# Attention values transposed twice, as fp32 and as fp32r from a DMA's copy, with the scaled difference added

## The chip, the cores and the metric

The kernel runs on one core of one Trainium2 chip, in one launch. The metric is the device time of that core in microseconds (us); lower is better. The core has five engines with queues of their own: PE (TensorE, matmuls; its weight loads are shown apart as PEld), DVE (VectorE), ACT (ScalarE), POOL (GpSimd) and SP (SyncE, which here only issues DMAs). Each engine takes its instructions strictly in the order of its queue and waits on semaphores for the others.

## The reference, cut to what matters

The program is one inference step of a two-layer hybrid encoder: layer 0 is a Mamba-2 mixer with a SwiGLU FFN, layer 1 is banded attention with a SwiGLU FFN. It is computed for 1024 prompt frames and 64 sample frames, which the kernel keeps side by side as 1088 columns. Only the attention of layer 1 matters here:

```python
kp, vp = shared_kv(xp, kv_norm_w, w_kv)          # rmsnorm(x) @ w_kv, split into K and V
qp = (rmsnorm(xp, nw[0]) @ attn_w_q[i]).reshape(bp, -1, ATT_HEADS, ATT_HEAD_DIM)
...
s = jnp.einsum('bqhd,bkhd->bhqk', q, k).astype(jnp.float32) * (ATT_HEAD_DIM ** -0.5) + bias
s = jnp.where(valid, s, -jnp.inf)
p = jax.nn.softmax(s, axis=-1).astype(v.dtype)
return jnp.einsum('bhqk,bkhd->bqhd', p, v)
```

There are 16 heads of 64 features. A query frame sees the frames of its own chunk of 64 and of the 8 chunks before it.

## The kernel before, in words

Everything is kept with features on the 128 partitions and frames along the free dimension. The 1088 columns are cut into three slices (SL) of 384, 384 and 320 columns. The 16 heads are taken as eight pairs j = 0..7; a pair's 128 features fill the partitions. Projections are done with split operands: each fp32 number is a rounded part (fp32r) and a rest, and a unit of projection (`unit`, `passes`, lines 533 to 535) is 8 steps of three matmuls, 24 in all, into one PSUM tile called mm.

For each pair j and slice s there are three units, K, V and Q. The function that empties a unit's PSUM tile is `evk` (line 1910: kf, then its rounded part on ACT and its rest on DVE, lines 1917 and 1918), `evv` (line 1964: vt) or `evq` (line 1936: qf). For V the values have to be turned, since the product of probabilities and values wants frames on the partitions: `v_task` transposes the three 128x128 blocks of vt on PE (line 1953, against the constant ident, into a PSUM tile vtp) and DVE copies the result to Vn (line 1954).

The attention itself goes in blocks of 128 queries, nine for each pair. A block has three steps, each placed by conditions of its own: the scores (lines 2001 and 2002, into PSUM tiles S; DVE adds the bias and finds the minimum at line 2011, ACT takes the exponential at 2016, DVE normalizes at 2017 and 2018), the transposition of the probabilities (line 2032, PSUM tiles ptp, copied out to pT at line 2036 by DVE for one head and ACT for the other), and, once for each slice, `values` (line 2067: po, the product with Vn, for three blocks in a row; ACT empties po at line 2075).

What sets the order. The program is written by a class `Stream` that counts planned time st.t while it writes PE's work: each matmul of a unit adds its planned cost, and side tasks (Python generators) yield a pair (cost, delay): the cost is added to st.t, and the task goes on when st.t has passed by the delay. So PE's queue is written out in full by the program, with attention steps put between the quarters of units. The instructions of the other engines are ordered by a scheduler with priorities: HIP (3000) for the emptying of units (lines 1909, 1935, 1963), ATP (1000) for the softmax steps and the copies to pT, and none for the copy to Vn.

Three resources matter below. The PSUM pool pax has two tiles with the tag ax, which `ax()` hands out in turn: vtp and po are such tiles. The pool nsb has tiles with the tags ssum (3 buffers) and sq (2 buffers), which the norms use before and after the attention. The tag kqv has four buffers, shared by kf, vt and qf. DMAs of the attention stage are all issued from SP's queue.

## Time and profile before

| what | value |
|---|---|
| median of 3 runs (lowest, highest) | 2895.07 us (2892.39, 2895.51) |
| the profiled execution's own time | 2895.43 us |
| its span (first to last instruction) | 2893.7 us |
| mean granted TensorE clock | 0.997 |
| busy PE, DVE, ACT, POOL | 2843.4, 2227.5, 1347.6, 772.8 us |
| attention stage | about 1594 us to 2060 us of the span |

The 1.7 us between the span and the execution's own time lie outside the first and the last instruction. In the rows of a timeline the first column is the start in us from the span's start, the second the duration; matmuls are pipelined, so that the distance from one start to the next, and not the duration, is what one costs. An entry in square brackets is the idle time of the engine before the row and what ended it. L1953 is line 1953 of the kernel.

### The profile page before, as it was taken

Reading aid. Unit: us, or ns where it says so; the run is one execution under the profiler, and the core shown is the slowest. Engines: PE = TensorE matmul, PEld = TensorE weight load, DVE = VectorE, ACT = ScalarE, POOL = GpSimd, SP = SyncE. Lnnn points to the kernel's source line nnn. Section 1 sums busy time; section 2 is a strip of 40 time slices with the busy share of each in tenths; the row PEclk is TensorE's granted clock in tenths of the full one; section 3 lists DMA queues with packets and bytes.
Section 4 is the critical chain, followed back from the end, with each engine's and each line's share of the span. In section 5 each row is a group of like instructions: output and inputs, shape, how many; then the busy total and the mean of one; then the engine's idle time right before and its main releaser. Section 6 shows DMA issues by size and latency. Waiting matters only on the chain. (4 is left out here: it accounts for less than half of the span.)

```text
span 2893.7 us, 57789 instructions
## 1 busy us (share of the span) xinstructions
PE 2843.4 (98%) x22096; PEld 2799.2 (97%) x22096; DVE 2227.5 (77%) x4739; ACT 1347.6 (47%) x2411; POOL 772.8 (27%) x971
## 2 busy tenths in 40 slices
PE   8999999999999999999999999999999999999999
PEld 8999999999999999999998899999999999999998
DVE  7887888886769877787677677777778877787456
ACT  6654646454454222235444555555564322234442
POOL 1343333330123434351024000000032434343012
PEclk9999999999999999999999999999999999999999
DMA  4433333235556555558875422223377454566555
GB/s 135 129 103 99 105 102 106 94 118 159 174 166 175 163 166 170 174 191 273 286 225 177 131 91 76 65 65 90 97 215 215 136 185 147 183 205 203 193 181 160
DMA packets 284791, 443.23 MB, mean 153 GB/s; under 512 B 25697, under 2 KB 231489, under 8 KB 283105
## 3 DMA queue, kind: packets, MB, share of 16 engines
q1 hardware_dynamic: 275232, 423.47, 45.6%
q0 software_dynamic: 3232, 10.56, 2.1%
q10 hardware_dynamic: 6048, 5.51, 0.6%
q8 instruction: 173, 2.83, 0.4%
q14 instruction: 106, 0.86, 0.1%
HBM read 321.34 MB, written 113.63 MB: 150 GB/s over the span
## 5 line engine op out<-in xcount | busy, mean ns | idle before, releaser
L533 PE MATMUL mm<-r,hl 128*128 128x384 f32 (+2 forms) x1672 | 556.2, 333 | 4.1 <-DMA hl<-kscr 2.4
L535 PE MATMUL mm<-r,hl 128*128 128x384 f32 (+2 forms) x1672 | 539.3, 323 | 1.2 <-DVE hl L389 0.7
L534 PE MATMUL mm<-r,hl 128*128 128x384 f32 (+2 forms) x1672 | 539.2, 322 | 0.0
L1428 PE MATMUL px<-r,hl 128*128 128x288 f32 (+1 forms) x1184 | 347.6, 294 | 0.0
L533 PEld LDWEIGHTS mm<-r,hl 128*128 128x128 f32 x1672 | 316.4, 189 | 6.1 <-DMA hl<-kscr 2.6
L535 PEld LDWEIGHTS mm<-r,hl 128*128 128x128 f32 x1672 | 315.3, 189 | 1.9 <-DVE hl L389 1.0
L534 PEld LDWEIGHTS mm<-r,hl 128*128 128x128 f32 x1672 | 316.2, 189 | 0.3
L1427 PE MATMUL px<-r,hl 128*128 128x288 f32 x1056 | 311.1, 295 | 2.8 <-DVE u L1448 1.6
L1429 PE MATMUL px<-r,hl 128*128 128x288 f32 x1056 | 311.4, 295 | 0.0
L389 DVE TENSOR_TENSOR hl<-raw,hl 128x1024 fp32r<-128x1024 f32 (+2 forms) x186 | 209.6, 1128 | 117.1 <-ACT hl L386 116.8
L559 POOL TENSOR_TENSOR ssum<-ssum,sq 128x256 f32<-128x256 f32 (+1 forms) x111 | 125.0, 1127 | 551.3 <-ACT sq L558 536.3
L386 ACT CAST hl<-raw 128x1024 fp32r<-128x1024 f32 (+2 forms) x186 | 177.5, 955 | 116.2 <-PE po L1770 72.3
L1428 PEld LDWEIGHTS px<-r,hl 128*128 128x128 f32 x1184 | 222.5, 188 | 0.0
L1429 PE MATMUL px<-rx,hl 128*128 128x256 f32 x768 | 214.9, 280 | 2.9 <-DVE hl L389 2.9
L1427 PE MATMUL px<-rx,hl 128*128 128x256 f32 x768 | 214.7, 280 | 0.9 <-DVE u L1442 0.9
L1427 PEld LDWEIGHTS px<-r,hl 128*128 128x128 f32 x1056 | 198.8, 188 | 4.6 <-DVE u L1448 2.0
L1429 PEld LDWEIGHTS px<-r,hl 128*128 128x128 f32 x1056 | 198.8, 188 | 0.1
L1768 PE MATMUL po<-r,hl 128*128 128x288 f32 (+1 forms) x682 | 196.7, 288 | 0.0
L1769 PE MATMUL po<-r,hl 128*128 128x288 f32 (+1 forms) x682 | 196.4, 288 | 0.0
L1770 PE MATMUL po<-r,hl 128*128 128x288 f32 (+1 forms) x682 | 196.4, 288 | 0.0
L1428 PE MATMUL px<-rx,hl 128*128 128x256 f32 x640 | 179.0, 280 | 0.0
L2016 ACT ACTIVATE sc<-sc,mx 128x640 f32<-128x640 f32 (+3 forms) x144 | 101.8, 708 | 106.3 <-DVE mx L2011 103.5
(450 smaller groups left out, 8428.9 us busy)
## 6 DMA issues: line engine op xcount, KB each, us to landing
raw<-in_w_f_dram SPq DMA_DIRECT2D x104, 512.0 KB, 4.0
wsum<-in_w_f_dram SPq DMA_DIRECT2D x128, 176.0 KB, 3.7
wscr<-wsum SPq DMA_DIRECT2D x128, 176.0 KB, 3.3
raw<-in_w_in_dram SPq DMA_DIRECT2D x40, 512.0 KB, 3.7
MT<-ascr SPq DMA_DIRECT2D x48, 384.0 KB, 4.3
raw<-in_w_so_dram SPq DMA_DIRECT2D x32, 512.0 KB, 3.8
r<-hscr SPq DMA_DIRECT2D x22, 576.0 KB, 6.0
hl<-kscr SPq DMA_DIRECT2D x11, 1024.0 KB, 6.1
```

Source lines behind the costliest of these rows:

```text
L386: last = self.nc.scalar.copy(h, v)
L389: (eng or self.eng or self.nc.vector).tensor_tensor(lo, v, h, op=ALU.subtract)
L533: PE.matmul(ps[:, :n], h_, xh, start=(first and i == 0), stop=False)
L534: PE.matmul(ps[:, :n], h_, xl, start=False, stop=False)
L535: at_pe[0] = PE.matmul(ps[:, :n], l_, xh, start=False, stop=(last and i == nk - 1))
L559: (eng or G).tensor_tensor(ssum[:, :n], ssum[:, :n], q[:, :n], op=ALU.add)
L1427: PE.matmul(ps, wh, ah[:, k, :], start=(k == 0), stop=False)
L1428: PE.matmul(ps, wh, al[:, k, :], start=False, stop=False)
L1429: at_pe[0] = PE.matmul(ps, wl, ah[:, k, :], start=False, stop=(k == 3))
L1768: PE.matmul(ps[:, :n], wh, xh, start=(k == 0), stop=False)
L1769: PE.matmul(ps[:, :n], wh, xl, start=False, stop=False)
L1770: at_pe[0] = PE.matmul(ps[:, :n], wl, xh, start=False, stop=(k == KH - 1))
```

## The change

Each `v_task` now also copies vt to a second tile vc by a DMA from SBUF to SBUF, waits 4.0 us of planned time, transposes vt as before, transposes vc once more with both operands taken as fp32r (with a copy of the identity matrix in fp32r, made once by ACT) into a second PSUM tile vtr, subtracts Vn from that on DVE, and adds the difference times 1048576 to Vn. The planned cost of a task goes from 0.33 to 0.55. There are 24 such tasks (eight pairs, three slices).

```diff
         def v_task(j, s, vt):
             Vn = kqv[j]["V"][s] = sb2.tile([P, 3, P], F32, tag="Vn", bufs=KBUF, name="Vn")
+            vc = nsb.tile([P, 384], F32, tag="ssum", bufs=3, name="vc")
+            nc.sync.dma_start(vc, vt)
+            if "ident" not in state:
+                state["ident"] = sb2.tile([P, P], F32R, tag="identr", bufs=1, name="identr")
+                A.copy(state["ident"], ident)
+            yield 0, 4.0
             pt = ax("vtp")
             for i in range(3):
                 PE.transpose(pt[:, i * P:(i + 1) * P], vt[:, i * P:(i + 1) * P], ident)
-            V.tensor_copy(Vn, pt[:, :3 * P].rearrange("p (a b) -> p a b", b=P))
-            yield 0.33, 0
+            flat = Vn.rearrange("p a b -> p (a b)")
+            V.tensor_copy(flat, pt[:, :384])
+            pt = ax("vtr")
+            for i in range(3):
+                PE.transpose(rr(pt[:, i * P:(i + 1) * P]), rr(vc[:, i * P:(i + 1) * P]), state["ident"])
+            df = nsb.tile([P, 384], F32, tag="sq", bufs=2, name="df")
+            V.tensor_tensor(df, pt[:, :384], flat, op=ALU.subtract)
+            V.scalar_tensor_tensor(flat, df, 1048576.0, flat, op0=ALU.mult, op1=ALU.add)
+            yield 0.55, 0
             v_done.append((j, s))
```

In the changed kernel the lines after these are 13 higher: 1954 (the copy to Vn) is now 1961, 1953 is 1959, the new transposition is 1964, the subtraction 1966, the scaled addition 1967; 2011 is 2024, 2018 is 2031, 2032 is 2045, 2067 is 2080.

Since the planned delay is longer, the tasks land at other places of PE's queue. PE's queue before, around the product po of a pair's first slice (12 rows of a projection unit stand ahead of the first row; ptp is the transposition of the next block's probabilities):

```order
L535 MATMUL mm<-r,hl 128x384
L2067 MATMUL po<-pT,Vn 64x128 x12
L2032 MATMUL ptp<-ident,sc 128x128 [waits DVE_49]
L2032 MATMUL ptp<-ident,sc 128x128 x3
L2032 MATMUL ptp<-ident,sc 128x128 [waits DVE_49]
L2032 MATMUL ptp<-ident,sc 128x128 x3
```

Here the product itself waits for nothing; the transposition of V for the next pair comes after it, six matmuls further on. PE's queue now, from that transposition on (vtp and vtr are the two transpositions, S the scores of the next block; between the last row here and the rows of the next fence stand the other scores and 12 matmuls of a unit):

```order
L1959 MATMUL vtp<-ident,vt 128x128 x2
L1959 MATMUL vtp<-ident,vt 128x128 [waits Pool_49]
L1964 MATMUL vtr<-identr,vc 128x128 [waits DMAHW0_49]
L1964 MATMUL vtr<-identr,vc 128x128 x2
L2014 MATMUL S<-K_24005,Qh_24388 128x320 [waits DVE_49]
```

The transpositions have moved ahead of the scores and of the product, and the second one waits for the DMA that fills vc. PE's queue now, at the product that follows:

```order
L535 MATMUL mm<-r,hl 128x384
L2080 MATMUL po<-pT,Vn 64x128 [waits DVE_49,PE_49]
L2080 MATMUL po<-pT,Vn 64x128 x11
L2045 MATMUL ptp<-ident,sc 128x128 x8
L533 MATMUL mm<-r,hl 128x384
```

The product has gained a wait on DVE: its PSUM tile is the one that vtp held, and the wait is for the copy from vtp to Vn. DVE's queue now, at that copy (ISA is the reduction over the scores S, with its second row reading the result; kf empties the K unit whose last 6 matmuls are the first 6 of the 12 fillers; L402 prepares weights):

```order
L2024 ISA sc,mx<-S,bias,mx 128x320 [waits DVE_49]
L2024 ISA mx 128x1
L2024 ISA sc,mx<-S,bias 128x320 [waits PE_49,Pool_49]
L2024 ISA mx 128x1
L1910 TENSOR_TENSOR kf<-mm,rbf 128x384 [waits PE_49]
L2024 ISA sc,mx<-S,bias,mx 128x320 [waits DVE_49]
L2024 ISA mx 128x1
L2030 RECIPROCAL mx<-mx 128x1 [waits Activation_49]
L402 SCALAR_TENSOR_TENSOR hl<-raw,pcs,hl 128x128
L2031 TENSOR_SCALAR sc<-sc,mx 128x640 [waits DVE_49]
L402 SCALAR_TENSOR_TENSOR hl<-raw,pcs,hl 128x128 x2
L1961 COPY Vn<-vtp 128x384
```

The copy stands behind the emptying of a unit that PE finishes only after the transpositions. This arrangement is found at five of the pairs: at three of them with the rows above, at two with two reductions and nothing else between kf and the copy.

## Prediction

> **What bounds the kernel now.** I read the page first, then the busy time by stage, then who waits for whom on PE, and last the timeline of PE and DVE around the steps that the change touches.

> ```profile
> span 2893.7 us, 57789 instructions
> PE 2843.4 (98%) x22096; PEld 2799.2 (97%) x22096; DVE 2227.5 (77%) x4739; ACT 1347.6 (47%) x2411; POOL 772.8 (27%) x971
> ...
> 1600.00:1700.00 100.00, 95.04 (x719) 91.34 (x719) 71.13 (x216) 49.78 (x114) 5.60 (x31) 0.98 0.36 117
> 1700.00:2060.00 360.00, 355.05 (x2868) 341.95 (x2866) 279.80 (x865) 213.89 (x524) 10.18 (x62) 1.00 0.26 79
> ```

> The first numbers of a stage's row are its length and then the busy time of PE, PEld, DVE, ACT and POOL. PE is busy for 98% of the whole and for 355 of the 360 us in which most pairs are done: PE's queue is the bound, and whatever is put into it, or makes it wait, is paid for. DVE has 80 us free in those 360. What little PE waits there is for DVE and ACT (columns: total, times, longest):

> ```profile
> PE S L2001 <- DVE mx L2011: 1.7, 4, 0.7
> PE S L2001 <- DVE pT L2036: 1.5, 2, 0.9
> PE ptp L2032 <- DVE mx L2011: 0.9, 2, 0.4
> PE S L2001 <- ACT pT L2036: 0.8, 2, 0.4
> ```

> These sum to 4.9 us, just the 360 less 355. The waits are short, so a delay of DVE by 1 us at the wrong place already reaches PE.

> **The change part by part.** *The second transposition on PE*: 24 tasks, three transpositions each, added to PE's queue. fp32r transpositions are not in this trace. From below I take the fp32 one of the same shape, from above the fp32r matmul of the same shape:

> ```profile
> 1858.66 0.31 PE L535 MATMUL mm<-r,hl 128*128 128x320 f32 x1
> 1858.81 0.49 PE L1953 MATMUL vtp<-ident,vt 128*128 128x128 f32 x3
> 1859.05 0.40 PE L533 MATMUL mm<-r,hl 128*128 128x320 f32 x1
> ...
> 1599.72 0.27 PE L2001 MATMUL S<-K,Qh 128*128 128x128 f32 x1
> ...
> 1599.95 0.36 PE L533 MATMUL mm<-r,hl 128*128 128x320 f32 x1
> ```

> Three fp32 transpositions take 1859.05 - 1858.81 = 0.24 us from start to start; two score matmuls of 128 columns take 0.23, so three would take 0.345. I take the middle, 0.29, since operand type speaks for the one and operation for the other: 24 x 0.29 = **+7.0 us** (5.8 to 8.3). Nothing hides it, as PE is the bound. [...]

> *The start of the stage.* In PE's queue two tasks now stand together ahead of the point where PE runs dry today:

> ```profile
> 1602.37 0.69 DVE L1882 TENSOR_TENSOR Ck<-cr,Ck 64x512 fp32r<-64x512 f32 x1 [0.68 <-ACT Ck L1881]
> ...
> 1605.96 0.41 PE L533 MATMUL mm<-r,hl 128*128 128x320 f32 x1 [2.35 <-DMA hl<-kscr]
> ```

> With two PSUM tiles, the second task's vtp needs the first's copy, and its vtr the first's subtraction. In DVE's queue that copy stands behind the Ck row above, which ends at 1603.06 because its data come by DMA. The copy (0.46, rows below), two short reductions (0.58 at most, at 0.29 each, an estimate from half of the 0.53 below) and the subtraction (0.47, like vt below) end at 1604.6. Then PE has three transpositions (0.29), four scores (0.46), 12 matmuls of 320 columns (12 x 0.15, row 1858.66 above) and a norm's three transpositions (0.24) ahead of the matmul that starts at 1605.96 today: 1607.4, or **+1.4 us**. The wait for hl disappears in this. Bounds: -0.6, if it all fits into the old wait (six transpositions that were ahead of it are now in it); +3, if Ck is later by half of the old wait.

> *The wait of po on DVE*, at five pairs. The rows of today around the same scores, 12 fillers and product give the times (PE, then DVE):

> ```profile
> 1869.79 0.31 PE L2001 MATMUL S<-K,Qh 128*128 128x320 f32 x1
> ...
> 1870.96 0.34 PE L533 MATMUL mm<-r,hl 128*128 128x384 f32 x1
> ...
> 1873.14 1.53 PE L2067 MATMUL po<-pT,Vn 128*64 128x128 f32 x24
> ```

> ```profile
> 1871.58 0.48 DVE L2011 CUSTOM_DVE_ANT_0 sc<-S,bias 128x320 f32<-128x320 f32 x1
> 1871.99 0.08 DVE L2011 DVE_READ_ACCUMULATOR2_ANT mx<- 128x1 f32 x1
> 1872.11 0.55 DVE L2011 CUSTOM_DVE_ANT_0 sc<-S,bias,mx 128x320 f32<-128x320 f32 x1
> ...
> 1872.71 0.17 DVE L2017 RECIPROCAL mx<-mx 128x1 f32<-128x1 f32 x1
> 1872.91 0.56 DVE L2018 TENSOR_SCALAR sc<-sc,mx 128x640 f32<-128x640 f32 x1
> 1873.38 0.55 DVE L1964 TENSOR_TENSOR vt<-mm,rbf 128x384 f32<-128x384 f32 x1
> 1873.85 0.15 DVE L2017 RECIPROCAL mx<-mx 128x1 f32<-128x1 f32 x1
> ```

> ```profile
> 1860.52 0.54 DVE L1954 COPY Vn<-vtp 128x384 f32<-128x384 f32 x1
> 1860.98 0.42 DVE L2018 TENSOR_SCALAR sc<-sc,mx 128x384 f32<-128x384 f32 x1
> ...
> 1865.52 1.14 DVE L402 SCALAR_TENSOR_TENSOR hl<-raw,pcs,hl 128x128 fp32r<-128x128 f32 x4
> 1866.57 0.68 DVE L2011 CUSTOM_DVE_ANT_0 sc<-S,bias 128x512 f32<-128x512 f32 x1
> ```

> ```profile
> 1598.50 0.34 PE L535 MATMUL mm<-r,hl 128*128 128x384 f32 x1
> ...
> 1598.87 0.56 DVE L1910 TENSOR_TENSOR kf<-mm,rbf 128x384 f32<-128x384 f32 x1 [1.32 <-PE mm L535]
> ```

> Count from the start of the scores. The fillers start at 1.17 and PE is at po at 3.35. kf needs the sixth filler, which starts at 1.17 + 5 x 0.175 = 2.04; kf follows 0.37 after such a start, at 2.41. Then DVE has, start to start: kf 0.47 (as vt), a reduction 0.53, reciprocal 0.20, scaling 0.47, three rows of L402 at 0.26, the copy 0.46. The copy ends at 5.33: PE waits 2.0 us. At the two pairs with two reductions and nothing else it ends at 2.41 + 0.47 + 1.06 + 0.46 = 4.40: 1.05 us. Sum 3 x 2.0 + 2 x 1.05 = **+8.1 us**. Bounds: 0, if DVE were not behind kf at all; +12, if DVE is already a reduction late at each. The copy has no priority, so kf and the reductions stay ahead of it. Behind the waiting po stand ptp and the next units, all of PE; DVE catches up during the wait.

> *Old waits that go.* In the new order there are 18 or 24 matmuls between scores and their transposition where 12 stood at the turn from a pair to the next, which is where the waits quoted above lie. I take half of the 4.9: **-2.5 us** (-4.9 to 0).

> *DVE's own added work*: 24 subtractions (0.47, as vt) and 24 scaled additions (no more than 0.55), 24 us into 80 free. Free time hides it; if it did not, it would be the 24. Where DVE is late already some shows: **+1 us** (0 to 6).

> *DMAs*: 24 issues on SP. SP waits at each for vt, which DVE writes at once (HIP); behind it stand Ql's copies and stores, whose sources DVE writes later than vt. The nearest transfer of that size:

> ```profile
> oscr<-ot SPq DMA_DIRECT2D x16, 192.0 KB, 1.9
> ```

> 1.9 us lie inside the planned 4.0, so 0 (0 to 24, if each came 1 us late). vt is held for those 4 us longer, of four kqv buffers; the units that take turns in them last longer than that. The identity's copy on ACT is one instruction, hidden by ACT's idle half.

> Sum: 7.0 + 1.4 + 8.1 - 2.5 + 1.0 = 15.0 us on the profiled execution's 2895.43 (its span of 2893.7 and 1.7 around it), 0.36 above the median. By the median: 2910 us.

> **The rivals.** (1) *No wait at po*: the copy gets through in time. Then the sum is 6.9, about 2902 us. For it speaks that today the same reductions end 0.5 us before po; against it that kf can't start before 2.41. Chance 0.18.

> (2) *The clock drops at these waits too.* After the wait of 2.35 us at 1605.96 the granted clock (last but two) is low:

> ```profile
> 1606.00:1608.00 2.00, 2.00 (x9) 2.00 (x10) 1.51 (x6) 1.16 (x4) 1.47 (x6) 0.61 0.98 409
> 1608.00:1610.00 2.00, 2.00 (x10) 2.00 (x9) 0.49 (x2) 0.00 (x0) 1.47 (x8) 0.54 0.12 45
> ```

> That is 2 x 0.39 + 2 x 0.46 = 1.7 us lost. If the three 2.0 us waits do the same it is +5.1, about 2915; at all five, 2919. The waits of up to 0.9 us quoted above did not (the clock of the 360 us is 1.00), so the point lies between. Chance 0.10. [...]

> (3) *Not slower.* The new order takes away all 4.9 us of the old waits and the 2.35 at the start with its 1.7 of clock: -8.95, against +7.0 of transpositions, with no wait at po: 2893.5, at least 2892.3 with transpositions at 5.8. It decides on DVE's copy being ahead of kf, and DVE's queue says the opposite. Chance 0.06.

> (4) *vc comes late*, because SP is held by an earlier wait: 24 us for 1 us each, 2934 in all with the rest. The order puts only short-lived waits ahead of vc. Chance 0.04.

> Whether the difference is zero changes no instruction, so no time.

> **How the numbers follow.** A measurement of this kernel can tell about 0.2% from no change, 5.8 us. The forecast (2906 to 2914) has 0.62. Slower by over 5.8 us: the forecast, rivals 2 and 4, and 0.11 of rival 1, whose value lies 1 us beyond the line, together 0.87. Within: the rest of rival 1 and most of rival 3, 0.12. Faster: 0.01. The range takes in rival 1 with its cheaper transpositions and half a microsecond of other savings more, 2899, and rival 2 with both kinds of waits and the dearest transposition, 2922; it leaves out rivals 3 and 4 and ends of the forecast.

> **What would show it.** Right: vtr at 0.24 to 0.345 us for three; a wait of PE at po for DVE's Vn, five times, 8 us; the wait for hl at the start replaced by one at vtp and vtr; stalls of S and ptp under 4.9 us. Wrong: PE waiting for vc's DMA, no wait at po, or a low clock after those waits.

## The result, and the profile after

The changed kernel takes 2916.24 us (median of three executions, 2913.01 to 2922.69) against 2895.07: a ratio of 1.0075, 95% interval 1.0058 to 1.0093, or 21 us more. The forecast was 2910.0, with a range of 2899 to 2922; the median lies 2 us above the band of 2906 to 2914 that had most of the chance. The profiled execution is the slowest of the three (2922.69 us), 27.2 us of span above the one shown of before; 4.9 us of these lie ahead of the attention stage, in code that did not change, so I read the stage by itself.

The page of the changed kernel, and its busy time by stage (columns as before: length, then PE, PEld, DVE, ACT, POOL; last but two the granted clock):

```profile
span 2920.9 us, 58057 instructions
PE 2856.4 (98%) x22168; PEld 2809.9 (96%) x22168; DVE 2249.9 (77%) x4787; ACT 1346.6 (46%) x2412; POOL 778.4 (27%) x971
```

```profile
1600.00:1700.00 100.00, 90.25 (x679) 86.05 (x678) 67.79 (x204) 44.28 (x103) 5.67 (x33) 0.97 0.42 133
1700.00:2060.00 360.00, 346.21 (x2753) 333.90 (x2750) 280.25 (x853) 202.88 (x495) 9.26 (x58) 0.99 0.26 80
```

PE's busy time grows by 13.0 us, and its free time grows too: it is 13.8 us of the 360 (4.9 before) and 9.8 of the first 100 (5.0 before). So the cost is of two kinds. Who PE waits for in the changed stage, 1570 to 2140 us (total, times, longest):

```profile
PE po L2080 <- DVE mx L2030: 7.0, 3, 2.5
...
PE po L2080 <- DVE Vn L1961: 4.0, 3, 1.8
PE vtp L1959 <- DVE Vn L1961: 3.5, 1, 3.5
PE mm L533 <- DMA hl<-kscr: 3.2, 1, 3.2
PE ptp L2045 <- DVE pT L2049: 1.9, 2, 1.3
...
PE S L2014 <- DVE mx L2024: 1.3, 3, 0.6
PE mm L533 <- DVE kf L1910: 1.2, 1, 1.2
...
PE S L2014 <- ACT pT L2049: 0.6, 2, 0.4
PE ptp L2045 <- DVE mx L2024: 0.5, 1, 0.5
PE S L2014 <- DVE pT L2049: 0.4, 1, 0.4
```

Waits of po, which did not exist before, are 11.0 us (the two rows for po; 10.65 of them at the five pairs, 0.35 at a sixth place). The row "mx L2030" is the same wait as "Vn L1961": it goes by the last event on DVE, and at three pairs a reciprocal ends just after the copy. Of S and ptp, 6.8 us of waits in the stage before, 4.7 are left (1.9 + 1.3 + 0.6 + 0.5 + 0.4). The rows of PE at the five pairs and at the start (duration after the start time, wait in brackets):

```profile
1609.40 0.90 PE L1959 MATMUL vtp<-ident,vt 128*128 128x128 f32 x3 [3.52 <-DVE Vn L1961]
...
1760.87 2.29 PE L2080 MATMUL po<-pT,Vn 128*64 128x128 f32 x24 [2.10 <-DVE mx L2030]
...
1827.58 1.53 PE L2080 MATMUL po<-pT,Vn 128*64 128x128 f32 x24 [1.84 <-DVE Vn L1961]
...
1892.73 1.53 PE L2080 MATMUL po<-pT,Vn 128*64 128x128 f32 x24 [1.81 <-DVE Vn L1961]
...
1957.01 1.53 PE L2080 MATMUL po<-pT,Vn 128*64 128x128 f32 x24 [2.45 <-DVE mx L2030]
...
2021.28 2.83 PE L2080 MATMUL po<-pT,Vn 128*64 128x128 f32 x24 [2.45 <-DVE mx L2030]
```

Two of the five products take 2.29 and 2.83 us instead of 1.53: the clock is down. After the other three, one of which waited just as long (2.45), it is not. DVE's queue at the first of them shows why po waits; PE was ready at 1760.87 - 2.10 = 1758.77:

```profile
1757.92 0.55 DVE L1910 TENSOR_TENSOR kf<-mm,rbf 128x384 f32<-128x384 f32 x1
1758.39 0.54 DVE L2024 CUSTOM_DVE_ANT_0 sc<-S,bias,mx 128x320 f32<-128x320 f32 x1
...
1758.93 0.33 DVE L402 SCALAR_TENSOR_TENSOR hl<-raw,pcs,hl 128x128 fp32r<-128x128 f32 x1
1759.18 0.55 DVE L2031 TENSOR_SCALAR sc<-sc,mx 128x640 f32<-128x640 f32 x1
1759.65 0.61 DVE L402 SCALAR_TENSOR_TENSOR hl<-raw,pcs,hl 128x128 fp32r<-128x128 f32 x2
1760.17 0.55 DVE L1961 COPY Vn<-vtp 128x384 f32<-128x384 f32 x1
```

The copy's data lay ready before the scores (the rows of vtp start at 1754.74 us, those of vtr at 1754.99, the scores at 1755.28); it is late by its place in the queue alone.

**An account that adds up.** For each profiled execution I take the span, less all waits of PE (the sum of the waits view), less half of PE's busy time in the stretches for which the profile's record of the granted clock says 0.5. What is left is work at full clock.

| profiled execution | span | waits of PE | lost at half clock | rest |
|---|---|---|---|---|
| before | 2893.7 | 44.5 | 8.5 | 2840.7 |
| before, once more | 2893.9 | 44.3 | 9.4 | 2840.1 |
| changed | 2920.9 | 59.3 | 14.4 | 2847.2 |
| changed, once more | 2916.8 | 60.4 | 8.2 | 2848.2 |

The rest is the same to 1 us in two executions of a kernel, and 7 us higher after the change (6.5 and 8.1), which fits the transpositions. Waits add 15 to 16 us. The third column differs by 6 us between two executions of one kernel; it is what scatters.

### The profile page after: what moved, and what is told of

It is laid out like the page before. It is cut to its first block, busy times and chain, and to the rows that moved or that the text cites. A ratio compares the mean times of both kernels' runs of the same rounds, so it can differ in the third digit from the quotient of the medians.

```text
span 2920.9 us, 58057 instructions
## 1 busy us (share of the span) xinstructions
PE 2856.4 (98%) x22168; PEld 2809.9 (96%) x22168; DVE 2249.9 (77%) x4787; ACT 1346.6 (46%) x2412; POOL 778.4 (27%) x971
## 5 line engine op out<-in xcount | busy, mean ns | idle before, releaser
L533 PE MATMUL mm<-r,hl 128*128 128x384 f32 (+2 forms) x1672 | 556.7, 333 | 5.3 <-DMA hl<-kscr 3.2
L535 PE MATMUL mm<-r,hl 128*128 128x384 f32 (+2 forms) x1672 | 539.1, 322 | 1.7 <-DMA hl<-in_w_in_dram 1.0
L533 PEld LDWEIGHTS mm<-r,hl 128*128 128x128 f32 x1672 | 316.6, 189 | 8.6 <-DMA hl<-kscr 3.5
L535 PEld LDWEIGHTS mm<-r,hl 128*128 128x128 f32 x1672 | 315.6, 189 | 2.3 <-DMA hl<-in_w_in_dram 1.3
```

Of the source, the lines that this page charges most:

```text
L533: PE.matmul(ps[:, :n], h_, xh, start=(first and i == 0), stop=False)
L535: at_pe[0] = PE.matmul(ps[:, :n], l_, xh, start=False, stop=(last and i == nk - 1))
```

## The experiments

Theory: PE's queue is the bound; the change costs 72 transpositions, waits of po for a copy that stands far back in DVE's queue, and a wait at the start of the stage. Rivals: DVE's 48 added instructions are the cost; the order is; the DMA is.

| kernel | us | ratio to before, 95% | lost to the clock | span less that |
|---|---|---|---|---|
| before (47 runs in three series) | 2894.31 to 2896.52 | | 8.8 | 2885.2 |
| changed (last columns: 4 runs) | 2916.24 | 1.0058 to 1.0093 | 9.5 | 2906.4 |
| order only | 2903.05 | 1.0015 to 1.0037 | 14.5 | 2886.9 |
| no DVE work | 2902.83 | 1.0017 to 1.0036 | 10.7 | 2890.7 |
| copy first | 2909.34 | 1.0034 to 1.0064 | 10.9 | 2896.9 |
| no delay | 2916.00 | 1.0051 to 1.0084 | 11.7 | 2902.6 |
| vtr three times | 2925.81 | 1.0094 to 1.0125 | 13.9 | 2910.6 |
| Ck on POOL, copy first | 2910.63 | 1.0039 to 1.0073 | 10.9 | 2898.1 |
| Ck on POOL, order only | 2901.77 | 1.0015 to 1.0037 | 13.3 | 2886.6 |
| Ck later, copy first | 2904.28 | 1.0019 to 1.0042 | 11.1 | 2892.0 |
| Ck later, order only | 2899.65 | 1.0005 to 1.0024 | 12.2 | 2885.8 |
| Ck later, kernel before | 2892.27 | 0.9978 to 0.9998 | 7.2 | 2883.7 |

The last two columns are means over the runs (4 to 10 of each changed program). Every run has its span and its mean granted clock on record, the clock to 0.001; the span times what the clock lacks to 1 is what the run lost to the clock. One run gives this to about 1.5 us, a mean more closely. It counts half-clock time in which PE waits as well, so it can lie above the account's figure.

### The order alone

```diff
-            vc = nsb.tile([P, 384], F32, tag="ssum", bufs=3, name="vc")
-            nc.sync.dma_start(vc, vt)
...
-            pt = ax("vtr")
-            for i in range(3):
-                PE.transpose(rr(pt[:, i * P:(i + 1) * P]), rr(vc[:, i * P:(i + 1) * P]), state["ident"])
-            df = nsb.tile([P, 384], F32, tag="sq", bufs=2, name="df")
-            V.tensor_tensor(df, pt[:, :384], flat, op=ALU.subtract)
-            V.scalar_tensor_tensor(flat, df, 1048576.0, flat, op0=ALU.mult, op1=ALU.add)
```

> Leaves out the copy by DMA, the second transposition, the subtraction and the scaled addition (which adds zero); keeps the planned delay of 4.0 and the cost of 0.55, so the V tasks stand where the changed kernel has them. Theory (PE's queue is the bound; the cost is 7 us of transpositions, waits of po for the copy, and the start): the order alone costs nothing, 2891 to 2897 us, no wait of po for DVE. Rival 'order': the later place of the tasks is itself the cost, 2905 or more with the waits still there.

Measured: 2903.05 us, 7.8 above the 2895.23 of before in the same series (0.15 to 0.37%). My theory fell here: no po waits, and yet a third of the change's cost. Two rows of PE and one of DVE in this kernel:

```profile
1604.49 0.39 PE L2003 MATMUL S<-K,Qh 128*128 128x256 f32 x1 [3.35 <-DVE mx L2013]
...
1640.41 0.69 PE L533 MATMUL mm<-r,hl 128*128 128x384 f32 x1 [3.83 <-DMA hl<-kscr]
```

```profile
1602.96 0.69 DVE L1882 TENSOR_TENSOR Ck<-cr,Ck 64x512 fp32r<-64x512 f32 x1 [2.36 <-ACT Ck L1881]
```

The start of the stage waits twice: for DVE, which stands at the subtraction for Ck until its DMA has come and ACT has rounded it, and 36 us later for weights from scratch memory. All its waits together are only 0.9 us more than before (45.4); but 17.2 us are lost at half clock in this execution, 8.7 more. Over the seven runs the loss is 5.8 us above that of the kernel before in the same series (14.5 to 8.7, give or take 3.5), and the span without it only 1.7 us longer. So most of the order's cost is lost clock: it costs by how its waits lie more than by their sum.

### Without DVE's added work

```diff
-            df = nsb.tile([P, 384], F32, tag="sq", bufs=2, name="df")
-            V.tensor_tensor(df, pt[:, :384], flat, op=ALU.subtract)
-            V.scalar_tensor_tensor(flat, df, 1048576.0, flat, op0=ALU.mult, op1=ALU.add)
```

> The changed kernel without DVE's subtraction and scaled addition (which add zero): vc's DMA and the second transposition stay, nothing reads vtr. Its PSUM tile is free at once, so po takes that one and needs no copy. Theory: 7 us of transpositions and 0 to 3 at the start on top of order_only, 2898 to 2906 us. Rival 'DMA': if vc's copies cost time this one keeps it, 2910 or more with PE waiting for vc.

Measured: 2902.83 us, within the theory's numbers, and the 24 DMAs cost nothing: no row of PE waits for vc. But it is no slower than "order only", though it has 72 transpositions more. In the account the rest grows by 5.1 us (2839.8 to 2844.9), and the loss at half clock is 7.4 smaller (17.2 to 9.8). The smaller loss is not only luck of these two executions: the means over ten and seven runs differ by 3.8 us (10.7 to 14.5, give or take 3.5), and without the loss this kernel is 3.8 us longer than "order only". So the transpositions do cost time here, and a smaller loss to the clock gives it back; why it is smaller, no run shows.

### The copy ahead of its neighbours

```diff
-            V.tensor_copy(flat, pt[:, :384])
+            with tc.high_priority(HIP):
+                V.tensor_copy(flat, pt[:, :384])
```

> The changed kernel with the copy from vtp to Vn at the priority of the evictions, so that it stands ahead of kf and of the reductions in DVE's queue; all the work is there. Theory: the waits of po (10.7 us in the changed kernel's trace) go to under 1, the clock drops behind them too, 8 to 12 us less than the changed kernel: 2903 to 2909. Rival 'DVE load': 48 added instructions of 0.55 us are what costs; the waits turn up elsewhere (S, ptp, evictions), 2912 or more.

Measured: 2909.34 us, 6.9 less than the changed kernel (by the two ratios 0.26%, give or take 0.23), just past the theory's range and short of the rival's. The waits of this kernel from 1600 to 2130 us:

```profile
PE vtp L1959 <- DVE Vn L1962: 4.4, 1, 4.4
PE mm L533 <- DMA hl<-kscr: 3.3, 1, 3.3
...
PE po L2081 <- DVE Vn L1962: 0.5, 1, 0.5
```

The waits of po have gone from 11.0 to 0.5: they are caused by the copy's place in DVE's queue. The whole gain did not come through: the start got dearer (4.4 instead of 3.5), and the runs lost 1.4 us more to the clock than those of the changed kernel. Without the clock the step is 9.5 us, near the 9.6 by which all waits shrank (59.3 to 49.7). Against "no DVE work" it is 6.5 us up (0.22%, give or take 0.18), with 4.6 us more of waits (49.7 against 45.1): both rivals held a part of the truth. But the kernel without DVE's work differs in one thing more, as nothing reads vtr there and po gets that PSUM tile at once; so the 6.5 us are not shown to be DVE's load alone.

### No delay

```diff
-            yield 0, 4.0
             pt = ax("vtp")
```

> The changed kernel without the planned delay of 4.0, so that the tasks stand about where the kernel before has them. Theory: fewer products meet the copy (by the order at two or three pairs), 7 us of transpositions stay: 2900 to 2908. Rival 'late vc': the second transposition now meets its DMA (0.5 us to issue and 2.1 to land), PE waits for vc at many of the 24 tasks, 2915 or more.

Measured: 2916.00 us, as slow as the changed kernel. The waits for vc came, but at two tasks only:

```profile
PE vtr L1963 <- DMA vc<-vt: 3.1, 2, 2.7
PE ptp L2044 <- DVE pT L2048: 3.1, 3, 1.3
...
PE S L2013 <- DVE mx L2023: 2.0, 2, 1.8
PE ptp L2044 <- DVE mx L2023: 1.8, 2, 1.2
...
PE vtr L1963 <- DVE df L1965: 1.2, 1, 1.2
```

The time is the rival's, the mechanism only in part: of 10.2 us of waits more than before (54.7 in all), 3.1 are for vc. Waits of ptp for DVE and ACT are 4.9 us more (6.4 after 1.5) and those of vtr 1.7, while those of S are fewer (4.0 after 5.3). Its rest, 2851.3, is also 10.6 above before, 3.6 more than the transpositions explain; where these lie I have not found.

### The second transposition three times

```diff
+            for i in range(3):
+                PE.transpose(rr(pt[:, i * P:(i + 1) * P]), rr(vc[:, i * P:(i + 1) * P]), state["ident"])
+            for i in range(3):
+                PE.transpose(rr(pt[:, i * P:(i + 1) * P]), rr(vc[:, i * P:(i + 1) * P]), state["ident"])
```

> The changed kernel with the second transposition done three times into the same PSUM tile: 144 more transpositions, nothing else, PE's order otherwise the same. Theory: PE's queue pays each of them, 48 groups of 0.29 us (start to start in the changed kernel's trace) = 13.9 us: 2927 to 2933. Rival 'hidden': the kernels with and without the second transposition (no_dve and order_only) took the same time, so it lies in time in which PE waits anyway: at most 5 us more, 2921 or less.

Measured: 2925.81 us, 9.6 more than the changed kernel (by the ratios 0.34%, give or take 0.23), between the two. One task of it on PE:

```profile
1784.34 0.46 PE L1964 MATMUL vtr<-identr,vc 128*128 128x128 f32 x3
1784.63 0.42 PE L1966 MATMUL vtr<-identr,vc 128*128 128x128 f32 x3
1784.88 0.42 PE L1968 MATMUL vtr<-identr,vc 128*128 128x128 f32 x3
1785.14 0.41 PE L533 MATMUL mm<-r,hl 128*128 128x384 f32 x1
```

From start to start the first three take 0.29 us, the next ones 0.25 and 0.26. So 48 more groups are 12.2 us (48 x 0.255), not 13.9. The waits shrank by 4.8 (59.3 to 54.5): a PE that arrives later waits less for DVE, and some of the added work goes into that. In the account the rest grows by about 9 us (2930.8 less 54.5 of waits and 19.8 at half clock is 2856.5). So the 9.6 us are made up of 4.2 us that are work less the waits it fills, about 9 less about 5, and of 4.4 us more lost to the clock (give or take 6). PE's queue pays for added transpositions, but the time alone does not show the full price: the rest grows by 3 us less than the 12.2, and what takes these up I have not found.

### Ck's subtraction on POOL

```diff
-                V.tensor_tensor(ch_[H2[1 - e], :], cr[H2[e], :], ch_[H2[e], :], op=ALU.subtract)
+                G.tensor_tensor(ch_[H2[1 - e], :], cr[H2[e], :], ch_[H2[e], :], op=ALU.subtract)
```

> copy_first with the subtraction for Ck on POOL instead of DVE, so that the first copy no longer stands behind a wait for Ck's DMA. Theory: the wait at the second vtp (4.4 us in copy_first) goes to under 1.5 us and one or both windows of half clock behind it go too: 2901 to 2906, against 2909 of copy_first. Rival: something else at that place is as late (the weights that come from scratch memory, the norm), and the time stays within 2 us of copy_first.

> order_only with the subtraction for Ck on POOL. Theory: the wait of S for the reduction (3.4 us, once) goes, and a window of half clock with it: 2896 to 2900, against 2903 of order_only. Rival: the order's cost lies in the later wait for the weights (3.8 us with two windows of half clock behind it), which stays: 2901 to 2904.

Measured: 2910.63 and 2901.77 us, both within 2 us of the kernel they start from; the rival's numbers. The first one's rows:

```profile
1605.15 0.55 PE L1959 MATMUL vtp<-ident,vt 128*128 128x128 f32 x3 [0.45 <-DVE Vn L1962]
...
1617.60 0.54 PE L604 MATMUL nbp<-ident,nr 128*128 128x128 f32 x3 [2.02 <-POOL nr L588]
```

The wait at vtp did go (4.37 to 0.45), but a norm that POOL prepares came 1.7 us later (2.02, where the changed kernel waits 0.33): my edit moved DVE's wait into POOL's queue. It settles nothing on the start, so I tried another way.

### Ck asked for later

```diff
-        load_side(0)
+        st.spawn(side_task(0))
...
-            yield 0, 0, lambda: cur["C"] >= 9 * j
+            yield 0, 0, lambda: cur["C"] >= max(9 * j, 1)
```

PE's order stays as it was in each of the three.

> copy_first with the load of the first pair's Ck (DMA, rounding on ACT, subtraction on DVE) asked for only after the first block's product, instead of ahead of everything; PE's order is unchanged and nothing moves to POOL, so the norm is not held up as in ck_pool. Theory (the start costs what DVE's wait for Ck's DMA costs): the wait of 4.4 us at the second vtp goes to under 1, with a window of half clock less: 2902 to 2906 us against 2909. Rival: the next late thing at that place (weights, norm) takes its place, within 2 us of 2909.

> order_only with the same later load of Ck. Theory: its 3.4 us wait of S for the reduction at the start goes: 2897 to 2901 against 2903, still slower than before by its later wait for weights. Rival: unchanged, 2901 to 2905.

> The kernel before with the same later load of Ck. In it DVE's wait for Ck lies beside PE's wait for the weights from scratch memory (2.35 us), so the theory expects no gain from DVE: 2893 to 2896. Rival: the two compete for the DMA engines, so the weights come earlier and the wait shrinks: 2889 to 2892, faster than both kernels.

Measured: 2904.28, 2899.65 and 2892.27 us: 5.1, 3.4 and 3 to 4 us less than without the edit. By the ratios the first is at the edge of what can be told from no change (0.19%, give or take 0.19), the second within it (0.11, give or take 0.15), and the last just outside (0.9978 to 0.9998); that all three go the same way speaks for one cause. The last is the fastest kernel here, ahead of both. The first of them at the second vtp, then the kernel before, once more, at its wait for the weights, then the same wait with Ck later:

```profile
1604.41 0.55 PE L1959 MATMUL vtp<-ident,vt 128*128 128x128 f32 x3 [0.65 <-DVE Vn L1962]
```

```profile
1608.25 0.64 PE L533 MATMUL mm<-r,hl 128*128 128x320 f32 x1 [3.36 <-DMA hl<-kscr]
```

```profile
1604.70 0.41 PE L533 MATMUL mm<-r,hl 128*128 128x320 f32 x1 [0.90 <-DMA hl<-kscr]
```

In the changed order the wait at vtp goes from 4.37 to 0.65 us, and the longest one for the weights from 3.3 to 1.2. In the kernel before I expected no gain, as DVE's wait lies beside PE's; the rival was right. Without Ck's loads beside it the load of the weights lands 5.60 us after its issue, where the kernel before, once more, takes 8.06, and the stretch at half clock behind that wait does not come at all.

### Both kernels once more

> The changed kernel, one more execution with its profile. Theory: what differs between executions of one kernel is the number of 3.413 us windows at half clock; span less PE's waits less half the windows' length was 2845.8 us, and comes out within 1.5 us of that again, with waits of po of 10 to 12 us again. Rival: the windows behind the waits of po are fixed to those waits: the same two of five have one.

> The kernel before, one more execution with its profile, to see what is the same between executions. Theory: span less PE's waits less half of PE's busy time in half-clock windows was 2840.7 us and comes out within 1.5 us again; windows at half clock follow where PE idles for 1.9 us or more of a 3.413 us stretch of the chip's own grid.

Measured: 2918.54 and 2895.59 us. The rests came out at 2848.2 and 2840.1 (the expectation for the changed kernel counted the loss over the whole stretches, by which it is 2845.9 after 2845.8). The five waits of po were 2.10, 1.81, 1.82, 2.50 and 2.37 us, and none of them was followed by a low clock: the stretches at half clock are not tied to these waits.

## Why the prediction was right, and where it was not

**The second transposition, +7.0 us: right.** In 22 of 24 tasks of the trace of after the three take 0.28 to 0.30 us from start to start, as taken. The rest in the account grew by 6.5 to 8.1. What I had not seen is that time in which PE waits takes up part of such work.

**The start, +1.4: the place right, the sum too small.** The wait for hl at the old place disappeared and the one at the second vtp took it over, 3.52 us for 2.35, +1.2. Not foreseen was the next one: 38 us later PE waits 3.2 us for the next weights, since in the new order the unit that frees their buffer lies too close ahead of the unit that needs them (the load is issued at 1642.09 us, as that unit ends, and lands 4.8 us later). With kf's (1.2 after 0.7) the start comes to 4.9 us, above its own bound of +3. The wait at vtp was also longer than the old Ck row let me think: Ck ended 3.50 us after the first scores before (1603.06 - 1599.56) and 4.90 after them now, its load being issued 0.7 us later in SP's queue and taking 0.7 longer.

**The waits of po, +8.1: right in kind, place and number, too small.** Five waits, 10.65 us at these pairs. Three of the 2.0 were 2.10, 2.45 and 2.45; the two of 1.05 were 1.84 and 1.81. The step that failed is that kf comes 0.37 us after the sixth filler. DVE's rows at the second pair:

```profile
1823.07 1.66 DVE L402 SCALAR_TENSOR_TENSOR hl<-raw,pcs,hl 128x128 fp32r<-128x128 f32 x6
1824.64 0.49 DVE L2024 CUSTOM_DVE_ANT_0 sc<-S,bias 128x320 f32<-128x320 f32 x1
...
1825.47 0.56 DVE L1910 TENSOR_TENSOR kf<-mm,rbf 128x384 f32<-128x384 f32 x1
```

Six rows of weights work keep it until 1824.64, and kf starts 3.22 us after the scores (1822.25), not 2.41. At the other four pairs it is 2.64, 3.20, 2.99 and 2.99 us: DVE was behind at all five, at four of them by a reduction or more, the case that I had put at the upper bound.

**Old waits that go, -2.5: right.** S and ptp in the stage: 6.8 us before (S 2.8, 1.7 and 0.8, ptp 0.9 and 0.6), 4.7 now, -2.1.

**DVE's added work, +1: too small.** "Copy first" against "no DVE work" gives 6.5 us, with an interval that reaches down to 1 (6.1 without the clock, and with the PSUM tile as a second difference). In the changed kernel part of it lies inside the waits of po.

**DMAs, 0: right** with the planned delay; without it two tasks wait 3.1 us.

**The clock, rival 2: not a rival but a part of every execution.** I tied it to the length of a wait; the low clock that I had named as a sign against the forecast came behind two of the five waits of po in one execution and behind none in the other. The sum of the terms as measured is 7.0 + 4.9 + 11.0 - 2.1 = 20.8 us with all of po's waits, near the median's 21.2. In the one profiled execution the clock adds 5.9, in the other it takes 0.3 off. Over all runs it adds 0.7 (9.5 after 8.8): the 21 us are work and waits, and the drops behind po that rival 2 priced at 5 to 9 us are not what they consist of, near as its 2915 comes.

What falls is the split. Undone step by step, the order alone is +7.8 us, of which the prediction had only a gain in old waits and the start; the transpositions on top of it did not show in the time (0 us, give or take 4), DVE's work is +6.5 and the place of the copy +6.9. These sum to the 21 us by construction, but each depends on what else is there. Without the loss to the clock (the last column of the table) the same four steps are +1.7, +3.8, +6.1 and +9.5, each give or take about 3.

That the median lies in the range is in part luck. The upper end of 2922 was put there for a clock that drops behind the waits of po; what filled it was a start and waits of po that were dearer than their terms, 3.5 and 2.9 us.

## What to carry to other kernels

Where one engine is full, count its added instructions, but then look in the other engine's queue for what its next operand stands behind: here a copy of 0.46 us with nothing urgent about it held a full PE for 2 us, and a priority on that one line gave 7 us back. A load that nothing needs yet (Ck) held back both a queue (the wait at the second vtp was 4.37 us with it and 0.65 without) and a transfer beside it (the weights landed 8.06 us after their issue with it and 5.60 without); asking for it later went with 3 to 5 us less in all three kernels, though each of these differences by itself is barely clear of noise or within it. When executions of one kernel differ, separate waits from clock before reading a difference of a few us.

## What the runs showed of the hardware

```profile
1758.06:1761.47 3.41, 1.31 (x16) 1.02 (x16) 3.36 (x12) 2.39 (x6) 0.00 (x0) 1.00 0.07 10
1761.47:1764.88 3.41, 3.41 (x27) 3.08 (x23) 2.69 (x5) 0.48 (x1) 0.00 (x0) 0.50 0.50 184
...
1952.62:1956.03 3.41, 1.94 (x12) 1.62 (x10) 3.41 (x14) 2.58 (x7) 0.00 (x0) 1.00 0.36 127
1956.03:1959.44 3.41, 2.43 (x33) 2.29 (x34) 3.30 (x9) 1.08 (x3) 0.00 (x0) 1.00 0.45 151
1959.44:1962.86 3.42, 3.42 (x26) 3.39 (x25) 1.51 (x3) 0.67 (x2) 0.00 (x0) 1.00 0.16 60
2017.47:2020.89 3.42, 1.35 (x8) 1.03 (x6) 3.42 (x14) 2.75 (x6) 0.00 (x0) 1.00 0.22 73
2020.89:2024.30 3.41, 3.02 (x25) 2.72 (x26) 3.00 (x7) 0.16 (x2) 0.00 (x0) 0.50 0.46 154
```

The waits of 2.10 and 2.45 us that leave PE busy for 1.31 and 1.35 us of one stretch are followed by a stretch at 0.50; the other wait of 2.45 is cut in two by a grid line (1.94 and 2.43 us busy), and the clock stays. Over all 14 profiles, from 100 us on and for stretches that were not at half clock themselves: with 1.9 us of waits or more in a stretch the next one was at half clock in 44 of 44 cases, with 0.9 to 1.2 us in none of 80, between 1.2 and 1.85 in 17 of 89 (a count near an edge moves by a few with the rounding of the grid). So a wait of 2 us costs 2.0 or 3.7 us (1.7 for half a stretch), by where the grid happens to lie; in "order only" a wait of 1.29 us with one of 0.36 behind it was followed by two such stretches. In these profiles a wait of a bit over half of such a stretch was enough (1.9 of 3.413 us). PE's idle time behind its last matmul is another matter: in the changed kernel's last whole stretch PE is busy for 1.48 of 3.41 us, and the 2.31 us to the end of the span are at 1.00.

**The first fp32r transpositions behind fp32 ones cost more than the next.** In the trace of the changed kernel three right behind the fp32 ones take 0.28 to 0.30 us from start to start (22 of 24 tasks), the fp32 ones 0.24 to 0.25 (23 of 24); further ones take 0.25 and 0.26 in the rows of "vtr three times". At that place the operand type, the source tile and the PSUM tile change together; which of them costs the 0.035 us no run separates.
